# A residual stream kept token-major in a two-block model kernel: w_out and w_down with X stationary, sums of squares on ScalarE, transposes for the next X

## The chip, the cores and the metric

The kernel runs as one program on one core of one Trainium2 chip. The metric is the time of one execution on the device in microseconds (us); of several runs the median counts. Engines are named as in the profile: PE is TensorE (matmuls), PEld its weight load, DVE VectorE, ACT ScalarE, POOL GpSimd, SP SyncE, which here issues the DMAs. Matmul results land in PSUM, which has eight banks of 128 partitions x 512 fp32; everything else that is worked on lies in SBUF.

## The reference

Two blocks run one after the other on 256 tokens of width 1024, in fp32. The first has two layers; each adds a mixer and a gated feed-forward net to the residual stream `h`, behind an RMS norm each time:

```python
def rms_norm(x, g):
    y = x * rsqrt(mean(x * x, axis=-1) + EPS)
    return y * g

# first block, for layer in range(2):
xn   = rms_norm(h, attn_norm_g[layer])
proj = xn @ w_in[layer]                       # u, u_g, v_g, q, k, v
mixed = concat([s5_mixer(u), spatial_gating(u_g, v_g), diff_attention(q, k, v)])
h = h + mixed @ w_out[layer]                  # 1024 x 1024
xn = rms_norm(h, ffn_norm_g[layer])
a  = xn @ w_up[layer]                         # 1024 x 5632
a  = causal depthwise conv of width 3 (a) ; gate, val = split(a)
h  = h + (gelu(gate) * val) @ w_down[layer]   # 2816 x 1024

# second block:
hn = rms_norm_2(h, g_pre)
# three branches (dilated-window, grouped-query and memory attention), each with
# a silu gate and a product w_br, merged by sigmoid gates
merged = g0 * ya + g1 * yb + g2 * ym
x = h + rms_norm_2(merged @ w_out_2, g_post)
```

## The kernel before, in words

Each fp32 operand of a large product is split into a high part (rounded to the fp32r format) and a low part (the rest), and each product is three matmuls: high x high, high x low, low x high. Weights come as a stream in the fixed order of use (`Stream`): SP loads a piece of up to 128 x 2048 into a `wraw` buffer (3 of them), ACT copies its high part (`whi`, line 152), DVE subtracts for the low part (`wlo`, line 153); 5 buffers of each hold pieces of 128 x 1024. `st.take()` hands out the next piece and starts the split of later ones.

The input of a product is called X and is kept feature-major: tiles `xh` and `xl` of [128, 8, 256], that is 8 groups of 128 features on the partitions and the 256 tokens along the free axis. The residual stream `h` has the same layout. A product comes in two forms. With the weights stationary (`gemm_ws256`, and the loops of w_out and w_down) a 128 x 128 block of weights is loaded and the 256 tokens of X move through; the result is feature-major. With X stationary (`gemm_xs512`, and the final w_out_2) a 128 x 128 block of X is loaded and 512 columns of weights move through; the result is token-major, with 128 tokens on the partitions. X is not yet divided by the norm: the product's result is multiplied afterwards by the reciprocal root `rstd` of each token's mean square (`rb`, the same as a row broadcast over all partitions by two matmuls, for feature-major results).

w_out and w_down accumulate into four PSUM banks (`acc`), each with two groups of 128 features x 256 tokens; the loop runs over the pieces of weights and, inside, over banks, halves and the three products. In layer 0 the banks of w_out are first filled with x itself, by 16 products of x (`xraw`, token-major as it comes from memory) with the identity. Other products use two `ps` banks; one bank each, `pt` and `px`, takes transposes, sums and small things.

`residual` (line 1201) follows each of the four products w_out and w_down. It goes through the four banks: DVE adds the bank to `h` (line 1209), ACT makes the high part of the next X, scaled by the norm's gain (line 667), DVE the low part (line 668), ACT squares, DVE adds the two halves, and PE sums over the features by a product with a column of ones (`Stats.add`). `norm_from` turns the sums into `rstd` and `rb`.

The second block takes its tokens in a permuted order. The gated activations of layer 1's feed-forward net are written permuted (`up`, with `last`), so that w_down's result comes out permuted, and `residual` with `permute` copies `h` permuted. In the second block `x2_gen` transposes `h` back to token-major (16 transposes, four ACT copies) for the last addition, and the output rows are written through the view `(c b a) d -> a b c d`, which undoes the permutation.

Order: the code is written in the order of the computation, generators (`fill`, advanced by `step()`) put work of other parts between the pieces of a product, and the tile framework's scheduler orders each engine's instructions by the priority of the code's order, weight splits pushed back by `split_later`. Each engine then runs its own list strictly in order, and waits by semaphores for the others. The DMAs of weights and of the output are in SP's list.

## Time and profile before

| | |
|---|---|
| median of 3 runs | 1060.17 us (1058.84 to 1060.65) |
| the profiled execution | 1058.25 us, its span 1056.5 us |
| mean granted TensorE clock | 0.993 of full speed |
| PE busy | 1008.0 us, 95% of the span, 7943 matmuls |
| PEld busy | 934.4 us, 88% |
| DVE busy | 778.8 us, 74%, 1577 instructions |
| ACT busy | 624.6 us, 59%, 1206 instructions |
| memory traffic | 160.15 MB read, 1.05 MB written, 153 GB/s over the span |

All durations of single instructions come from the one profiled execution, which is 1.75 us longer than its span of work. Busy time of PE overlaps from one matmul to the next, since matmuls are pipelined, so the distance between starts (the pitch) tells what one costs. A window gives the busy time of each engine in a stretch; where PE's is as long as the window, PE never waits there. The chain of waits is followed back from the last instruction to what released each one.

### The profile page before, as it was taken

What the parts mean: (1) busy time and instruction counts of PE and PEld (TensorE: products, weight loads), DVE (VectorE), ACT (ScalarE), POOL (GpSimd) and SP (SyncE); (2) the same over time, 40 slices, a digit from 0 to 9 for tenths busy, and PEclk for the clock granted to TensorE, in tenths of its full rate; (3) what the DMA queues carried; (4) which work ended last, traced back from release to release, by engine and by line L of the source; (5) the groups of instructions that cost most, each with busy time, mean ns of one, the idle gap of its engine ahead of it and who ended that gap; (6) DMA issues with size and microseconds to landing.
All of it is one profiled execution on the core that took longest, in us unless ns stands there. A gap on an engine that the chain in (4) does not pass through costs nothing.

```text
span 1056.5 us, 20003 instructions
## 1 busy us (share of the span) xinstructions
PE 1008.0 (95%) x7943; PEld 934.4 (88%) x7943; DVE 778.8 (74%) x1577; ACT 624.6 (59%) x1206; POOL 14.3 (1%) x34
## 2 busy tenths in 40 slices
PE   6799899999999999998999999999999999999994
PEld 4678899999999988888999999998787899899993
DVE  6989869987888678768878778875565776456663
ACT  4886567656675577757555545646565545444450
POOL 2000000000000000000000000000000000000000
PEclk9999999999999999999999999999999999999997
DMA  6543253556555553253465656468323445325531
GB/s 191 194 160 132 71 187 107 176 191 220 182 186 171 182 169 122 80 193 127 161 202 172 206 172 203 138 196 282 108 98 110 148 144 188 117 90 194 174 126 40
DMA packets 130485, 166.68 MB, mean 158 GB/s; under 512 B 12034, under 2 KB 103256, under 8 KB 130392
## 3 DMA queue, kind: packets, MB, share of 16 engines
q1 hardware_dynamic: 130360, 165.40, 47.7%
q8 instruction: 62, 1.02, 0.4%
q14 instruction: 31, 0.25, 0.1%
q10 hardware_dynamic: 32, 0.01, 0.0%
HBM read 160.15 MB, written 1.05 MB: 153 GB/s over the span
## 4 chain that ended last, share of the span: by engine, by line
PE 79%; DVE 4%; ACT 3%; issue 1%; SPq 0%; DMA 0%; POOL 0%; ACTq 0%; POOLq 0%
PE acc L94 47%; PE ps L94 26%; DVE wlo L153 1%; PE pt L1509 1%; ACT whi L152 1%; PE px L94 1%; PE acc L1564 1%; PE acc L1655 1%; DVE sgen L409 1%; ACT sgen L600 1%; DVE gen L1334 0%; ACT gen L1008 0%; DVE gen L1336 0%; DVE gen L409 0%; PE acc L1566 0%
## 5 line engine op out<-in xcount | busy, mean ns | idle before, releaser
L152 ACT ACTIVATE whi<-wraw 128x1024 fp32r<-128x1024 f32 x294 | 307.9, 1061 | 231.5 <-PE acc L94 110.8
L153 DVE TENSOR_TENSOR wlo<-wraw,whi 128x1024 fp32r<-128x1024 f32 x294 | 356.6, 1223 | 102.1 <-ACT whi L152 99.4
L94 PE MATMUL ps<-xh,whi 128*128 128x256 f32 x736 | 208.7, 285 | 3.7 <-DVE gen L1345 3.4
L94 PE MATMUL ps<-xl,whi 128*128 128x256 f32 x736 | 208.2, 284 | 0.8 <-DVE xl L668 0.8
L94 PE MATMUL ps<-xh,wlo 128*128 128x256 f32 x736 | 207.9, 283 | 0.0
L94 PE MATMUL acc<-xh,wlo 128*128 128x256 f32 x672 | 193.6, 289 | 4.3 <-DVE wlo L153 4.3
L94 PE MATMUL acc<-xh,whi 128*128 128x256 f32 x672 | 194.4, 291 | 1.1 <-ACT vm L1198 0.7
L94 PE MATMUL acc<-xl,whi 128*128 128x256 f32 x672 | 193.4, 288 | 0.1
L94 PEld LDWEIGHTS ps<-xh,whi 128*128 128x128 f32 x736 | 140.5, 191 | 4.4 <-DVE gen L1345 1.9
L94 PEld LDWEIGHTS ps<-xl,whi 128*128 128x128 f32 x736 | 140.9, 192 | 1.1 <-DVE xl L668 1.0
L94 PEld LDWEIGHTS ps<-xh,wlo 128*128 128x128 f32 x736 | 140.9, 192 | 0.0
L94 PEld LDWEIGHTS acc<-xh,wlo 128*128 128x128 f32 x672 | 129.1, 192 | 6.5 <-DVE wlo L153 5.3
L94 PEld LDWEIGHTS acc<-xh,whi 128*128 128x128 f32 x672 | 129.0, 192 | 4.5 <-issue 1.3
L94 PEld LDWEIGHTS acc<-xl,whi 128*128 128x128 f32 x672 | 129.0, 192 | 2.4 <-issue 1.5
L94 PE MATMUL acc<-whi,xh 128*128 128x512 f32 (+1 forms) x352 | 125.1, 357 | 2.9 <-ACT xh L667 2.4
L94 PE MATMUL acc<-wlo,xh 128*128 128x512 f32 (+1 forms) x352 | 125.2, 356 | 1.7 <-DVE wlo L153 1.6
L94 PE MATMUL acc<-whi,xl 128*128 128x512 f32 (+1 forms) x352 | 124.2, 354 | 0.0
L94 PE MATMUL acc<-al,whi 128*128 128x256 f32 x352 | 99.0, 281 | 0.5 <-DVE al L672 0.5
L94 PE MATMUL acc<-ah,whi 128*128 128x256 f32 x352 | 99.1, 282 | 0.0
L94 PE MATMUL acc<-ah,wlo 128*128 128x256 f32 x352 | 98.6, 281 | 0.0
L94 PEld LDWEIGHTS acc<-whi,xh 128*128 128x128 f32 x352 | 67.1, 191 | 11.6 <-ACT xh L667 3.3
L94 PEld LDWEIGHTS acc<-wlo,xh 128*128 128x128 f32 x352 | 67.1, 191 | 10.4 <-DVE wlo L153 2.6
(348 smaller groups left out, 1517.2 us busy)
## 6 DMA issues: line engine op xcount, KB each, us to landing
wraw<-in_w_in_dram SPq DMA_DIRECT2D x58, 1024.0 KB
wraw<-in_w_up_dram SPq DMA_DIRECT2D x44, 1024.0 KB
wraw<-in_w_down_dram SPq DMA_DIRECT2D x22, 1024.0 KB
wraw<-in_w_out_dram SPq DMA_DIRECT2D x12, 1024.0 KB
wraw<-in_w_mem_kv_dram SPq DMA_DIRECT2D x4, 1024.0 KB
gen<-gen SPq DMA_DIRECT2D x48, 64.0 KB
wraw<-in_w_br_b_dram SPq DMA_DIRECT2D x2, 1024.0 KB
wraw<-in_w_br_m_dram SPq DMA_DIRECT2D x2, 1024.0 KB
```

What stands on the lines that cost most here:

```text
L94: self.nc.tensor.matmul(out, lhsT=lhsT, rhs=rhs, start=not self.open if start is None else start, stop=stop)
L152: self.nc.scalar.activation(hv, part, AF.Copy)
L153: self.nc.vector.tensor_tensor(lv, part, hv.bitcast(F32), op=OP.subtract)
L409: (eng or V).tensor_tensor(o, a, b_, op=op)
L600: A.copy(pd[ps, hf], bpow[ri][ps, a * 4 : a * 4 + 4])
L1509: T.transpose(bk.t[:, i * P : (i + 1) * P], p[:, i * P : (i + 1) * P], ident)
L1564: T.matmul(oc, lhsT=pt[:, kt * P : (kt + 1) * P], rhs=vs[0][:, kt, cols], start=kt == 0, stop=False)
L1655: T.matmul(oc, lhsT=pt[:, (i * 2 + kt) * P : (i * 2 + kt + 1) * P], rhs=vb[:, kt, kv * 64 : kv * 64 + 64], start=kt == 0, stop=kt == 1)
```

## The change

The residual stream stays token-major in `xraw`, where x is loaded, seen as `xrv`: 128 tokens on the partitions, two halves of tokens q, 1024 features. For this

- w_out and w_down are computed with X (the mixer's output, or the gated activations) stationary and 512 columns of weights moving (`mm_tok`); the four banks are two halves of tokens x two halves n of the features;
- `residual` adds each bank into `xrv` (DVE), squares with the row sum taken by the same ACT instruction, and makes the next feature-major X by 16 transposes on PE, from which ACT and DVE write the high and low parts, reading PSUM. The transposes go four at a time into the banks `pt` and `px` in turn;
- the products with ones, the products of x with the identity, and `x2_gen` are gone, and the last addition reads `xrv`;
- the permutation is made in the last residual, by transposes that write PSUM with a stride (`tokens`), with two more transposes for the norm; the gated activations are no longer permuted; the last merge adds with a permuted view, so that the product w_out_2 and the output are in the plain order, and each half of the output is one store of 128 rows in place of two of 64 rows in permuted order;
- `merged` moves from the pool of `h` to another, and the final store's view changes with it.

The core of the diff:

```diff
-    def norm_from(ss):
+    def tokens(ap, q, permute):
+        if not permute:
+            return ap[:, q * P : (q + 1) * P]
+        return flat_view(ap)[:, :, :, q * 8 : q * 8 + 8].rearrange("p a b c -> p c b a")
+
+    def norm_from(ss, permute=False):
...
-            T.matmul(bk.t[:, q * P : (q + 1) * P], lhsT=rstd[:, q : q + 1].to_broadcast([P, P]), rhs=ident,
+            T.matmul(tokens(bk.t[:, :S], q, permute), lhsT=rstd[:, q : q + 1].to_broadcast([P, P]), rhs=ident,
...
+        if permute:
+            bk = pst()
+            for q in range(2):
+                T.transpose(bk.t[:, q * P : (q + 1) * P], rb[:, q * P : (q + 1) * P], ident)
+            rstd = small.tile([P, 2], F32, name=nm("rstd"), tag="rstd", bufs=2)
+            A.copy(rstd, bk.t[:, :S].rearrange("p (q c) -> p q c", q=2)[:, :, 0])
...
-    def residual(banks, h, gcol, X, stats, permute=False, new=False):
-        for bi in range(4):
-            ks = slice(bi * 2, bi * 2 + 2)
-            hs = h[:, ks, :].rearrange("p k s -> p (k s)")
-            if new:
-                hv = banks[bi].t
-            else:
-                hv = gen() if permute else hs
-                V.tensor_tensor(hv, banks[bi].t, hs, op=OP.add)
-            for n in range(2):
-                k, x_ = bi * 2 + n, hv[:, n * S : (n + 1) * S]
-                split_scaled(X[0][:, k, :], X[1][:, k, :], x_, pcol(gcol + k))
-                if permute:
-                    A.copy(flat_view(h[:, k, :]), perm_view(x_))
-            sq = gen()
-            A.activation(sq, hv, AF.Square)
-            stats.add(sq)
-            if new:
-                A.copy(hs, hv)
+    def residual(banks, h, gcol, X, permute=False):
+        parts = sm(4)
+        for n in range(2):
+            for q in range(2):
+                hv = h[:, q, n * 512 : n * 512 + 512]
+                tt(hv, banks[q][n].t, hv, OP.add)
+                A.activation(gen(), hv, AF.Square, accum_out=parts[:, q * 2 + n : q * 2 + n + 1])
+            for kp in range(2):
+                bk = psx() if kp else pst()
+                for kk in range(2):
+                    k = n * 4 + kp * 2 + kk
+                    for q in range(2):
+                        T.transpose(tokens(bk.t[:, kk * S : (kk + 1) * S], q, permute), h[:, q, k * P : (k + 1) * P], ident)
+                for kk in range(2):
+                    k = n * 4 + kp * 2 + kk
+                    split_scaled(X[0][:, k, :], X[1][:, k, :], bk.t[:, kk * S : (kk + 1) * S], pcol(gcol + k))
...
+    def mm_tok(banks, rows, last):
+        for n in range(2):
+            cols = slice(n * 512, n * 512 + 512)
+            for i, (xh, xl, hi, lo) in enumerate(rows):
+                for q in range(2):
+                    tok = slice(q * P, (q + 1) * P)
+                    b = banks[q][n]
+                    b.mm(b.t, xh[:, tok], hi[:, cols])
+                    b.mm(b.t, xh[:, tok], lo[:, cols])
+                    b.mm(b.t, xl[:, tok], hi[:, cols], stop=last and i == 1)
...
-        banks = [acc() for _ in range(4)]
-        if l == 0:
-            for k in range(8):
-                for q in range(2):
-                    banks[k // 2].mm(banks[k // 2].t[:, (k % 2) * S + q * P : (k % 2) * S + (q + 1) * P],
-                                     xrv[:, q, k * P : (k + 1) * P], ident)
-            h = hpool.tile([P, 8, S], F32, name="h0", tag="h")
...
+        banks = [[acc(), acc()] for _ in range(2)]
+        for k in OUT_ORDER[l]:
+            rows = []
+            for kk in range(2):
+                hi, lo = st.take()
+                rows.append((mix[0][:, k + kk, :], mix[1][:, k + kk, :], hi[:, 0, :], lo[:, 0, :]))
+            mm_tok(banks, rows, k == OUT_ORDER[l][-1])
+            step(2)
...
-    fill.append(x2_gen())
...
-                    tt(mv, mv, y, OP.add)
+                    if bi_ == 2:
+                        mt = gen()
+                        for n in range(2):
+                            sl = slice(n * S, (n + 1) * S)
+                            tt(perm_view(mt[:, sl]), flat_view(mv[:, sl]), flat_view(y[:, sl]), OP.add)
+                        mv = mt
+                    else:
+                        tt(mv, mv, y, OP.add)
...
-    ov = out[0].rearrange("(c b a) d -> a b c d", b=4, a=4)
+    ov = out[0].rearrange("(q p) d -> q p d", p=P)
...
-        V.scalar_tensor_tensor(of, of, rs, x2[:, q], op0=OP.mult, op1=OP.add)
-        for al in range(2):
-            nc.sync.dma_start(ov[q * 2 + al], of[al * 64 : al * 64 + 64, :])
+        V.scalar_tensor_tensor(of, of, rs, xrv[:, q], op0=OP.mult, op1=OP.add)
+        nc.sync.dma_start(ov[q], of)
```

How the instructions stand on the engines is shown at two places. The first is the handover from w_out of layer 1 to the up-products that follow. Names: `acc` are the banks of w_out, `ps` those of the up-products, `xh` and `xl` the parts of X, `gen` scratch tiles, `ident` the identity. A row is line, operation, result and operands, shape, and how many in a row. On PE, before, from the last w_out matmul on:

```order
L94 MATMUL acc_5745<-xh_5441,wlo_5863 128x256
L94 MATMUL ps_6056<-xh_5978,whi_5892 128x256
L94 MATMUL ps_6124<-xh_5978,whi_5950 128x256
L94 MATMUL ps_6056<-xl_5979,whi_5892 128x256
...
L94 MATMUL ps_6124<-xh_5978,wlo_5951 128x256
L94 MATMUL px_5980<-ones,gen_5989 128x1 x2
L94 MATMUL ps_6056<-xh_5978,whi_5892 128x256
L94 MATMUL ps_6124<-xh_5978,whi_5950 128x256
```

On PE, after:

```order
L94 MATMUL acc_5386<-whi_5455,xl_5083 128x512
L1208 MATMUL pt_5532<-ident,xraw 128x128 x4
L1208 MATMUL px_5541<-ident,xraw 128x128 x4
L94 MATMUL ps_5599<-xh_5523,whi_5461 128x256
L94 MATMUL ps_5667<-xh_5523,whi_5495 128x256
L94 MATMUL ps_5599<-xl_5524,whi_5461 128x256
...
L94 MATMUL ps_5667<-xh_5523,whi_5495 128x256
L1208 MATMUL pt_5556<-ident,xraw 128x128 x4
L1208 MATMUL px_5565<-ident,xraw 128x128 x4
L94 MATMUL ps_5599<-xl_5524,whi_5461 128x256
```

The products with ones stood one pair at a time between the up-products; now two sets of eight transposes stand there, the second behind the eighth matmul of the up-products, into the same two banks as the first.

On DVE at the same place, before, from the first add of a w_out bank on:

```order
L1209 TENSOR_TENSOR gen_5981<-acc_5742,h_1637 128x512
L153 TENSOR_TENSOR wlo_6058<-wraw_5890,whi_6057 128x1024
L668 SCALAR_TENSOR_TENSOR xl_5979<-gen_5981,pvt,xh_5978 128x256 x2
L1209 TENSOR_TENSOR gen_5994<-acc_5743,h_1637 128x512
L409 TENSOR_TENSOR gen_5989<-gen_5989 128x256
L153 TENSOR_TENSOR wlo_6088<-wraw_5948,whi_6087 128x1024
L668 SCALAR_TENSOR_TENSOR xl_5979<-gen_5994,pvt,xh_5978 128x256 x2
L1209 TENSOR_TENSOR gen_6007<-acc_5744,h_1637 128x512
L409 TENSOR_TENSOR gen_6002<-gen_6002 128x256
L668 SCALAR_TENSOR_TENSOR xl_5979<-gen_6007,pvt,xh_5978 128x256 x2
```

And after, from the first add on (`xraw` is the stream):

```order
L407 TENSOR_TENSOR xraw<-acc_5383,xraw 128x512
L407 TENSOR_TENSOR xraw<-acc_5385,xraw 128x512
L407 TENSOR_TENSOR xraw<-acc_5384,xraw 128x512
L153 TENSOR_TENSOR wlo_5601<-wraw_5459,whi_5600 128x1024
L407 TENSOR_TENSOR xraw<-acc_5386,xraw 128x512
L666 SCALAR_TENSOR_TENSOR xl_5524<-pt_5532,pvt,xh_5523 128x256
L666 SCALAR_TENSOR_TENSOR xl_5524<-px_5541,pvt,xh_5523 128x256
L153 TENSOR_TENSOR wlo_5631<-wraw_5493,whi_5630 128x1024
L666 SCALAR_TENSOR_TENSOR xl_5524<-pt_5532,pvt,xh_5523 128x256
L666 SCALAR_TENSOR_TENSOR xl_5524<-px_5541,pvt,xh_5523 128x256
```

The four adds now come together, with one weight split among them, and the four low parts that are read from the first two transpose banks follow around a second weight split.

The second place is after w_down of layer 0, where the products of the memory keys (`ps` with `wlo`) stand between the residual and the first product of layer 1 (`acc` with `whi`). On PE, before, from the last product of the memory keys on:

```order
L94 MATMUL ps_4590<-xh_3486,wlo_4532 128x256
L94 MATMUL px_4652<-ones,gen_4658 128x1 x2
L94 MATMUL px_4652<-ones,gen_4668 128x1 x2
L94 MATMUL px_4652<-ones,gen_4678 128x1 x2
L94 MATMUL px_4652<-ones,gen_4688 128x1 x2
L94 MATMUL acc_4712<-whi_4561,xh_4650 128x512
L94 MATMUL acc_4712<-wlo_4562,xh_4650 128x512
```

On PE, after:

```order
L94 MATMUL ps_4221<-xh_3261,wlo_4163 128x256
L1208 MATMUL pt_4290<-ident,xraw 128x128 x4
L1208 MATMUL px_4299<-ident,xraw 128x128 x4
L94 MATMUL acc_4353<-whi_4192,xh_4281 128x512
L94 MATMUL acc_4353<-wlo_4193,xh_4281 128x512
...
L94 MATMUL acc_4354<-whi_4192,xh_4281 128x512
L1208 MATMUL pt_4314<-ident,xraw 128x128 x4
L1208 MATMUL px_4323<-ident,xraw 128x128 x4
L94 MATMUL acc_4353<-whi_4192,xl_4282 128x512
```

All products with ones stood ahead of the first wide matmul; now the first eight transposes do, and the second eight stand behind the ninth of the wide matmuls.

## Rows read from the trace of the kernel before

**Rows 1.** The page: busy time of PE; shares of the chain that ended last.
```profile
PE 1008.0 (95%) x7943; PEld 934.4 (88%) x7943; DVE 778.8 (74%) x1577; ACT 624.6 (59%) x1206; POOL 14.3 (1%) x34
...
PE 79%; DVE 4%; ACT 3%; issue 1%; SPq 0%; DMA 0%; POOL 0%; ACTq 0%; POOLq 0%
```

**Rows 2.** Windows: stretch, length, busy us (x instructions) per engine, clock, DMA share, GB/s.
```profile
472.00:490.00 18.00, 14.79 (x116) 13.85 (x114) 14.29 (x31) 13.75 (x23) 0.00 (x0) 1.00 0.42 142
490.00:656.50 166.50, 166.28 (x1393) 166.31 (x1394) 133.38 (x192) 93.59 (x121) 0.00 (x0) 1.00 0.54 181
669.00:708.00 39.00, 39.00 (x328) 38.59 (x326) 29.29 (x54) 20.23 (x29) 0.00 (x0) 1.00 0.58 174
```

**Rows 3.** Timeline of DVE and SP at the end; windows of the end and of x's load.
```profile
1043.94 1.28 DVE L1812 SCALAR_TENSOR_TENSOR o<-o,sm,x 128x1024 f32<-128x1024 f32 x1
1039.82 6.55 SPq L1814 DMA_DIRECT2D out_dram<-o  x4
...
1040.00:1041.00 1.00, 0.67 (x3) 0.20 (x2) 0.00 (x0) 0.30 (x1) 0.00 (x0) 1.00 0.00 0
1046.00:1055.00 9.00, 0.00 (x0) 0.00 (x0) 0.00 (x0) 0.00 (x0) 0.00 (x0) 0.50 0.24 86
1.70:6.50 4.80, 0.73 (x2) 0.36 (x2) 1.93 (x1) 0.77 (x1) 4.49 (x12) 1.00 0.79 299
```

**Rows 4.** Chain in order of time: start us, us, engine tile line xcount.
```profile
361.42 7.54 PE acc L94 x33
...
605.09 5.68 PE acc L94 x48
610.77 11.51 PE ps L94 x96
```

**Rows 5.** Timeline of PE, last 24 matmuls: first and last (start us, us, instruction).
```profile
1035.07 0.39 PE L94 MATMUL acc<-whi,xh 128*128 128x512 f32 x1
...
1040.28 0.39 PE L94 MATMUL acc<-whi,xl 128*128 128x512 f32 x1
```

**Rows 6.** Lines of PE: xcount | busy us, mean ns | idle before.
```profile
L94 PE MATMUL px<-ones,gen 128*128 128x1 f32 x64 | 8.1, 237 | 0.0
...
L94 PE MATMUL acc<-ident,xraw 128*128 128x128 f32 x32 | 4.6, 282 | 0.0
```

**Rows 7.** Timeline of PE, eight transposes of the x2 step and the next matmul.
```profile
680.85 1.09 PE L1443 MATMUL pt<-ident,h 128*128 128x128 f32 x8
681.70 0.36 PE L94 MATMUL acc<-xh,wlo 128*128 128x256 f32 x1
```

**Rows 8.** Lines of DVE and ACT that the handovers use.
```profile
L1209 DVE TENSOR_TENSOR h<-acc,h 128x512 f32<-128x512 f32 x8 | 5.3, 682 | 0.0
L668 DVE SCALAR_TENSOR_TENSOR xl<-ps,pvt,xh 128x256 fp32r<-128x256 f32 x8 | 3.6, 476 | 0.1
L153 DVE TENSOR_TENSOR wlo<-wraw,whi 128x1024 fp32r<-128x1024 f32 x294 | 356.6, 1223 | 102.1 <-ACT whi L152 99.4 <-PE pt L696 0.8
...
L667 ACT ACTIVATE xh<-ps,pvt 128x256 fp32r<-128x256 f32 x8 | 3.4, 469 | 1.0 <-PE ps L800 0.8 <-DVE xl L668 0.2
L1193 ACT COPY kmT<-ps 128x512 f32<-128x512 f32 x2 | 1.1, 567 | 0.0
```

**Rows 9.** Timeline of PE at two handovers; in brackets the wait and its releaser.
```profile
141.04 0.28 PE L94 MATMUL ps<-xh,whi 128*128 128x256 f32 x1
...
157.74 0.38 PE L94 MATMUL ps<-xh,whi 128*128 128x256 f32 x1 [1.68 <-DVE gen L1345]
...
471.75 0.40 PE L94 MATMUL ps<-xh,whi 128*128 128x256 f32 x2
...
490.22 0.35 PE L94 MATMUL ps<-xh,whi 128*128 128x256 f32 x1 [1.74 <-DVE gen L1345]
```

**Rows 10.** Windows: the one place inside the work where the clock fell.
```profile
41.00:45.00 4.00, 0.04 (x1) 0.00 (x0) 4.00 (x11) 3.83 (x10) 0.00 (x0) 0.95 0.08 22
45.00:48.00 3.00, 2.97 (x14) 2.97 (x15) 3.00 (x7) 2.96 (x16) 0.00 (x0) 0.50 0.01 3
```

More of the change, by code (lines that the diff above doesn't have):

```diff
@@ L1290, in layer @@
         low[0] = 0
[L1291 to L1310 removed]
+        banks = [[acc(), acc()] for _ in range(2)]
[6 more added lines that the diff above has]
+            step(2)
         last = l == LAYERS - 1
         X = new_x()
[L1313 to L1316 removed]
+        rstd, rb = residual(banks, h, FG + l * 8, X)
         rb2 = rb.unsqueeze(1).to_broadcast([P, 2, S])
         st.split_later = (SPLIT_F0, SPLIT_F1)[l]
[L1320 removed]
+        banks = [[acc(), acc()] for _ in range(2)]
         if not last:
@@ L1349, in up @@
             ac = gen()
-            if last:
-                for n in range(2):
-                    sl = slice(n * S, (n + 1) * S)
-                    tt(flat_view(ac[:, sl]), perm_view(g_[:, sl]), perm_view(v_[:, sl]), OP.mult)
-            else:
-                tt(ac, g_, v_, OP.mult)
+            tt(ac, g_, v_, OP.mult)
             ah = work.tile([P, 512], F32R, name=nm("ah"), tag="mid", bufs=5)
@@ L1363, in down @@
             subs = [st.take(), st.take()]
[L1364 to L1373 removed]
+            rows = []
+            for kk in range(2):
+                hi, lo = subs[kk]
+                sl = slice(kk * S, (kk + 1) * S)
+                rows.append((ah[:, sl], al[:, sl], hi[:, 0, :], lo[:, 0, :]))
+            mm_tok(banks, rows, j == 10)
             step()
@@ L1385, in layer @@
         Xo = new_x()
-        stats = Stats()
-        residual(banks, h, GP if last else AG + 8, Xo, stats)
-        return h, Xo, stats.finish()
+        return Xo, residual(banks, h, GP if last else AG + 8, Xo, last)
     def chain(*gs):
@@ L1396, in tile_model @@
     for l in range(LAYERS):
-        h, X, norm = layer(l, None if l == 0 else h, X, norm)
+        X, norm = layer(l, xrv, X, norm)
     b1.close()
@@ L1433, in tile_model @@
     V.tensor_scalar(rstdh, rstd, 0.5, None, op0=OP.mult)
-    x2 = const2.tile([P, 2, D], F32, name="x2")
-    def x2_gen():
-        for q in range(2):
-            for half in range(2):
-                bk = pst()
-                for k in range(4):
-                    T.transpose(bk.t[:, k * P : (k + 1) * P], h[:, half * 4 + k, q * P : (q + 1) * P], ident)
-                A.copy(x2[:, q, half * 512 : half * 512 + 512], bk.t)
-                yield
     def qt_tile():
```

47 lines of the change are left out of this document (5 added, 42 removed).

## The prediction

> **What bounds the kernel now.** I read the page's busy shares and the chain of waits first: TensorE (PE) is busy 95% of the span and holds 79% of the chain [rows 1]. The windows by stretch then say where it is not the limit. In the feed-forward stretch and at the start of the second block PE never waits, while VectorE (DVE) has a fifth of its time free [rows 2]. So a nanosecond taken from a matmul there shows in the time. PE loses time in three kinds of place. One is the mixers' own waits. The second is the handover from one product to the next: after w_out of layer 1, 18 us hold 14.79 us of PE work [rows 2]. The third is the end: the last DVE instruction is over at 1045.2 and the span ends at 1056.5, with PE idle [rows 3]. The sum below is made against the profiled execution, 1058.25 us; the median of the runs, 1060.17, lies 1.9 above it, and that is added at the end.
>
> **Width of the two products.** In w_out and w_down 256-column matmuls become half as many 512-column ones. The chain gives the pitch of the old form: 48 w_down matmuls in 5.68 us, 118.3 ns each; 96 of the same form in 11.51 us, 119.9 ns [rows 4]. The new form (X stationary, weights moving) exists already: the last 24 matmuls of the kernel start 23 pitches apart in 5.21 us, 226.5 ns, and a run of 33 amid busy DVE and ScalarE (ACT) took 7.54 us, 228.5 ns [rows 4, 5]. So a pair gives back 2 x 118.3 - 228.5 = 8 ns in w_down and 11 in w_out: the columns streamed stay the same, and only a fixed part of some 10 ns is paid once instead of twice. Pairs: w_down 2 layers x 11 x 24 = 528, w_out 2 x 96 = 192. 528 x 8.1 + 192 x 11.3 = 4.3 + 2.2 = 6.5 us, all on the path. Bounds: 0, if the wide form goes at 237 ns beside the splits; 8, at 226.5.
>
> **Removed from PE.** In layer 0 the 16 products with the identity that load x into the w_out banks (32 records, 4.6 us busy [rows 6], about 0.11 us apart) go. Most stood where PE waits for the attention chain anyway, so I count 2.0 us of 3.5 (bounds 1 and 3.5). The sums of squares by a ones column (64 records, 8.1 us busy [rows 6]) and the 16 transposes of the old x2 step go too; eight of these in a row took 0.85 us up to the next matmul, 0.106 us apiece [rows 7]. They are set against what the handovers gain.
>
> **Added, at the four handovers.** Each gets 16 transposes, 16 x 0.106 = 1.7 us, against 16 records of sums of squares, about the same; so the count is even and what matters is waiting. PE takes its instructions in the written order. The second eight transposes write into the same two PSUM banks as the first eight, so they wait until DVE has read four tiles out, and the rest of the next product is queued behind them, as is everything that reads it. After the last w_out matmul of layer 1 DVE still has one add (0.68), a weight split (1.22), two low parts (0.48 each), a weight split and two more low parts, as the order shows: 0.68 + 1.22 + 0.95 + 1.22 + 0.95 = 5.0 us [rows 8]. ACT's high parts (0.47 each [rows 8]) run beside. The second transposes then end near 5.5 us, and PE has done only 8 matmuls of the next product meanwhile. The other 88 take 10.5 us, the row sums' broadcast 0.2: 16.2 us until the third up-product can begin.
> - After w_out, layer 0: now 141.04 to 157.74, 16.7 us [rows 9]. Gain 0.5.
> - After w_out, layer 1: now 471.75 to 490.22, 18.5 us, the last 1.74 of it a wait for the norm's user on DVE, with the norm itself delayed by the ones products [rows 9]. The squares now come off ACT with their sum, eight copies of h are gone, and the norm is ready before the first bank is full. Gain 2.3.
> - After w_down, layer 0: the 96 matmuls of the memory keys stand ahead of all 16 transposes. An ACT copy of keys (0.57), a high and a low part [rows 8] stand before the first wide matmul may take its operands, some 1.4 us of which the first transposes cover 0.9. That costs 0.5; the next transposes find their banks read out, as four high parts and a low part end by 3.2 us. Loss 0.5.
> - After w_down, layer 1: PE does not wait today [rows 2]. 12 matmuls and 16 records, 3.2 us, become 5.5; two more transposes for the permuted norm 0.2; the old x2 transposes give back 1.7. Loss 0.8.
> Together a gain of 1.5. Bounds: a loss of 8 (2 us more at each place) to a gain of 7 (no waiting). The trace has no transpose that writes PSUM with a stride; the nearest row is the plain one, and I take 0.106; at four times that, the 18 strided ones would add 5.8.
>
> **A rule against the change.** The granted clock fell to 0.5, the 1.2 GHz level, in one place inside the work: PE was idle from 41 to 45, and from 45 to 48 it got through 14 matmuls where 25 would fit, a loss of about 1.3 us [rows 10]. In the gaps around 472 to 490 it stayed at 1.00 [rows 2]. The Trainium skill, "TensorE: Matmul & The Clock Gate", part 4 on transposes, says that transposes do not count as PE activity the way matmuls do; by it the handovers, now transposes and short waits, could drop the clock. The trace leaves this open, as no stretch of it holds mainly transposes; it is rival C.
>
> **Costed at nothing.** DVE's 16 adds replace 12 adds and 16 pair sums; ACT loses four copies of x2, eight permuted copies and four of h. DVE's free fifth in the feed-forward stretch covers the rest; uncovered, the four extra accumulator reads per handover would cost under 1 us each. Eight half-width permuted adds replace four full ones in the last merge, beside PE's gate products; uncovered, 4 x 0.7.
>
> **The end.** Now: the last scaling ends at 1045.2, SyncE (SP) issues the second pair of output DMAs, packets run through the whole of 1046 to 1055 at a DMA share of 0.24 and 86 GB/s, and the span ends at 1056.5: 11.3 us [rows 3]. A share of 0.24 is four of 16 engines. The order of the output rows is 4 x 4 x 16 there; after the change a store is 128 plain rows, as the loads of x are, and the stretch of those loads shows a share of 0.79 and 299 GB/s [rows 3]. So 512 KB take 1.75 us instead of the queue of 1 MB. From issue (1039.82) to the first packet pass 1.2 us (none before 1041) [rows 3], and 1.5 from the last packet to the end: 1.2 + 1.75 + 1.5 = 4.5. Gain 6.8. Bounds: 0, if a store to memory goes at 86 GB/s whatever its shape; 7, at four times 86.
> The Trainium skill, "DMA: Bandwidth & Descriptors", section on why a DMA increments its semaphore by 16, says that a transfer uses the largest number of engines up to 16 that divides the slowest dimension of both sides: 4 before, 16 after. The 0.24 agrees; the sum by this rule is the one I made from rows.
>
> **Sum.** 6.5 + 2.0 + 1.5 + 6.8 = 16.8. 1058.25 - 16.8 = 1041.4, and with the 1.9 of the runs 1043.4 us.
>
> **Rivals.** A: the store is limited by the memory and not by four engines; for it, all of the trace's wide transfers are loads. The gain falls to 10: 1050. B: the wide matmuls gain nothing, since the trace's chain of them is often interleaved and DVE writes weight parts at the same time; against it, the 33 at 228.5. 1050. C: the clock drops at each handover, 4 x 1.3: 1049. D, the slower side: in-order PE stands still behind the two transpose banks for the whole preparation of X. If none of it is hidden, a handover costs two adds 1.4, 16 transposes 1.7, eight high and low parts 7.6, two weight splits 2.4, 13.1 instead of 5.5, four times 7.6 more: 1074. It turns the sign from 4.7 us more per handover on. For it, these places hold little else for PE to do; against it, the first half's transposes and matmuls stand ahead, and the last matmuls of the first product (12 wide ones, 2.7 us) cover the first adds. E: neither the width nor the store does what it should and the handovers lose a few us: no change, 1058 to 1062.
>
> **Numbers.** Forecast 0.74 (its own range 1039 to 1048), A 0.08, B 0.06, C 0.05, D 0.04, E 0.03. The range to 1052 takes in A, B and C with the median's own spread of 1; below, no waiting at the handovers and 8 from the width give 1036 to 1037, and it begins at 1037. A measurement of this kernel tells about 0.2% from no change, 2 us. Faster 0.93, the same 0.03, slower 0.04.
>
> **What would show it.** The page: 720 fewer matmuls from the wide form, all w_down rows 128x512 at a pitch of 227 to 230. The windows: the wait for the norm in the up stretch of layer 1 gone, and a new one on PE ahead of the second transposes, released by DVE's low parts, of 1 to 3 us at each of three handovers. Granted clock 1.00 there. At the end, two stores, a DMA share far above 0.24, and 4 to 5 us from the last DVE instruction to the end of the span. Wrong it would be if the store still took 9 us, if the wide matmuls came at 236 ns, or if the waits ahead of the second transposes passed 5 us.

## The result

The changed kernel took 1048.46 us, the median of 4 runs (1047.36 to 1049.75), beside 1059.51 for the kernel before in the same comparison: 0.9896 of it, interval 0.9877 to 0.9915. Forecast were 1043.4 and a range of 1037 to 1052: 11.0 us faster instead of 16.8, two thirds of the forecast gain. The profiled execution took 1047.36, its span 1045.1, against 1058.25 and 1056.5 before.

PE's busy line and its share of the chain, which answer to [rows 1]:

```profile
PE 1001.7 (96%) x7177; PEld 893.2 (85%) x7177; DVE 772.0 (74%) x1561; ACT 618.0 (59%) x1207; POOL 14.5 (1%) x34
...
PE 82%; DVE 8%; ACT 6%; issue 2%; DMA 1%; SPq 0%; POOL 0%; ACTq 0%; DVEq 0%; POOLq 0%
```

766 matmul records fewer: 720 from the wide form, 64 sums of squares, 32 loads of x and 16 transposes of the x2 step gone, 66 transposes new. The columns streamed by the large products are the same in both traces, so each place of the work can be set against the same place in the other trace. The table gives when it is reached (us from the start of the span), what the stretch in front of it gained or lost, and the terms of the forecast that belong there (2.2 for w_out and 4.3 for w_down halved over the layers):

| up to | before | after | stretch | forecast |
|---|---|---|---|---|
| end of w_out, layer 0 | 141.04 | 139.77 | -1.3 | -3.1 |
| third up-product, layer 0 | 157.74 | 157.20 | +0.7 | -0.5 |
| end of w_down, layer 0 | 344.5 | 342.5 | -1.5 | -2.15 |
| layer 1's first products behind the residual | 369.0 | 367.8 | +0.8 | +0.5 |
| end of w_out, layer 1 | 471.75 | 470.30 | -0.2 | -1.1 |
| third up-product, layer 1 | 490.22 | 486.93 | -1.8 | -2.3 |
| end of w_down, layer 1 | 668.6 | 664.1 | -1.2 | -2.15 |
| last 24 matmuls | 1035.1 | 1031.1 | +0.5 | +0.8 |
| end of the span | 1056.5 | 1045.1 | -7.4 | -6.8 |

The end. The last scaling on DVE, the second store on SP, and the windows behind them; they answer to [rows 3]:

```profile
1039.94 1.29 DVE L1789 SCALAR_TENSOR_TENSOR o<-o,sm,xraw 128x1024 f32<-128x1024 f32 x1
1041.26 0.34 SPq L1790 DMA_DIRECT2D out_dram<-o  x1
```

```profile
1041.20:1042.00 0.80, 0.00 (x0) 0.00 (x0) 0.03 (x1) 0.00 (x0) 0.00 (x0) 0.50 0.00 0
1042.00:1044.10 2.10, 0.00 (x0) 0.00 (x0) 0.00 (x0) 0.00 (x0) 0.00 (x0) 0.50 0.64 254
```

From the end of DVE's instruction (1041.23) to the end of the span pass 3.9 us, not 11.3. No packet moves up to 1042; then the store is through within 2.1 us at a share of 0.64, before at 0.24. (Columns of windows as in [rows 2].)

The wide matmuls, which answer to [rows 4, 5]. Chain of waits (start, length, tile, count), one w_down step and the up-products before it; then PE's timeline, first and last of six matmuls of w_out in layer 1 and of twelve of w_down:

```profile
214.29 11.51 PE ps L94 x96
225.80 5.60 PE acc L94 x24
```

```profile
462.81 0.39 PE L94 MATMUL acc<-whi,xh 128*128 128x512 f32 x1
...
463.95 0.39 PE L94 MATMUL acc<-whi,xl 128*128 128x512 f32 x1
...
603.42 0.39 PE L94 MATMUL acc<-wlo,ah 128*128 128x512 f32 x1
...
605.99 0.40 PE L94 MATMUL acc<-whi,ah 128*128 128x512 f32 x1
```

w_out: (463.95 - 462.81) / 5 = 228 ns. w_down: (605.99 - 603.42) / 11 = 233.6, and 5.60 / 24 = 233.3. The same form through the same function comes 6 ns later in w_down. A pair there gives back 2 x 118.4 - 233.4 = 3.4 ns, not 8.1.

The handovers. PE at the one behind w_out of layer 0 and at the one of layer 1, from the first transposes to the third up-product (469.61 is the third last matmul of w_out); they answer to [rows 9]:

```profile
139.77 0.60 PE L1208 MATMUL pt<-ident,xraw 128*128 128x128 f32 x4
140.20 0.60 PE L1208 MATMUL px<-ident,xraw 128*128 128x128 f32 x4
142.11 0.50 PE L94 MATMUL ps<-xh,whi 128*128 128x256 f32 x2 [1.31 <-ACT xh L665]
...
144.06 0.50 PE L94 MATMUL ps<-xh,whi 128*128 128x256 f32 x2 [0.69 <-ACT xh L665]
144.67 0.63 PE L1208 MATMUL pt<-ident,xraw 128*128 128x128 f32 x4
...
157.20 0.36 PE L94 MATMUL ps<-xh,whi 128*128 128x256 f32 x1
...
469.61 0.39 PE L94 MATMUL acc<-whi,xh 128*128 128x512 f32 x1
...
470.30 0.60 PE L1208 MATMUL pt<-ident,xraw 128*128 128x128 f32 x4
...
472.02 0.50 PE L94 MATMUL ps<-xh,whi 128*128 128x256 f32 x2 [0.68 <-ACT xh L665]
472.74 0.38 PE L94 MATMUL ps<-xl,whi 128*128 128x256 f32 x1 [0.21 <-DVE xl L666]
...
473.97 0.50 PE L94 MATMUL ps<-xh,whi 128*128 128x256 f32 x2 [0.50 <-ACT xh L665]
474.74 0.63 PE L1208 MATMUL pt<-ident,xraw 128*128 128x128 f32 x4 [0.27 <-DVE xl L666]
475.21 0.60 PE L1208 MATMUL px<-ident,xraw 128*128 128x128 f32 x4
...
486.93 0.28 PE L94 MATMUL ps<-xh,whi 128*128 128x256 f32 x1
```

Two waits were in the forecast, the second transposes (DVE's low parts, 0.27 at 474.74) and what is queued behind them; they end at 145.6 and 475.6, 5.8 and 5.3 us after the first transposes began, forecast 5.5. But the wait of 1 to 3 us ahead of the second transposes, looked for at three handovers, is 0.27 at this one and nothing at the other three. A third wait was not in the forecast: PE has nothing between the first transposes and the first matmul that reads them, and waits 1.31 and 0.68 us for ACT's first high part, and again 0.69 and 0.50 for the second pair; at the handovers behind w_down it is 1.00 and 0.69. From the end of w_out to the third up-product it is 17.4 and 16.6 us; forecast were 16.2 for both.

The granted clock at the four handovers, and the window of layer 1 that stood in [rows 2]:

```profile
139.50:146.00 6.50, 4.37 (x30) 3.42 (x29) 6.09 (x14) 5.53 (x14) 0.00 (x0) 1.00 0.58 197
353.50:359.00 5.50, 4.50 (x30) 3.78 (x29) 2.89 (x6) 3.65 (x8) 0.00 (x0) 1.00 0.60 192
470.00:476.00 6.00, 4.34 (x30) 3.38 (x29) 5.80 (x14) 4.76 (x12) 0.00 (x0) 1.00 0.52 193
664.00:670.50 6.50, 5.37 (x39) 4.42 (x38) 6.30 (x15) 5.22 (x13) 0.00 (x0) 1.00 0.49 160
472.00:490.00 18.00, 16.93 (x134) 16.18 (x135) 13.93 (x31) 12.59 (x23) 0.00 (x0) 1.00 0.45 152
```

1.00 at each in this run. It was not so in every run. In three experiments below whose handovers hold the same instructions, the profiled run shows the clock at 0.50, the 1.2 GHz level, at one handover: in `pad_after` and `odd_x` behind w_out of layer 1 (473 to 476 and 475 to 478), in `ident_load` behind w_out of layer 0 (144 to 147). In `pad_before`, which is the kernel before with a pad, it fell at two, behind the second up-product of layer 0 and behind w_out of layer 1. `pad_after` ahead of the fall and in it, then the two falls of `pad_before`:

```profile
470.00:473.00 3.00, 1.67 (x8) 1.13 (x8) 3.00 (x6) 2.89 (x9) 0.00 (x0) 0.99 0.50 124
473.00:476.00 3.00, 2.64 (x13) 2.59 (x13) 1.98 (x9) 1.05 (x3) 0.00 (x0) 0.50 0.55 225
```

```profile
158.00:161.00 3.00, 3.00 (x16) 3.00 (x16) 3.00 (x8) 2.28 (x5) 0.00 (x0) 0.50 0.23 69
479.00:482.00 3.00, 3.00 (x17) 3.00 (x16) 1.88 (x4) 2.37 (x5) 0.00 (x0) 0.52 0.00 0
```

In `pad_after` the stretch from the first transposes to the third up-product took 17.8 us (468.91 to 486.69) where the changed kernel took 16.6: the fall cost about 1.1 us. The Trainium skill, "TensorE: Matmul & The Clock Gate", part 4 on transposes, says that a transpose does not count as PE activity the way a matmul does. No run here tells that apart from the waits that stand beside the transposes; the kernel before does not transpose the stream at its handovers, and in `pad_before` the clock fell there too. The window of 472 to 490 now holds 16.93 us of PE work in 18, before 14.79.

### The profile page after: what moved, and what is told of

Read it like the earlier page. It is cut to its first block, busy times and chain, and to the rows that moved or that the text cites. A ratio compares the mean times of both kernels' runs of the same rounds, so it can differ in the third digit from the quotient of the medians.

```text
span 1045.1 us, 18439 instructions
## 1 busy us (share of the span) xinstructions
PE 1001.7 (96%) x7177; PEld 893.2 (85%) x7177; DVE 772.0 (74%) x1561; ACT 618.0 (59%) x1207; POOL 14.5 (1%) x34
## 4 chain that ended last, share of the span: by engine, by line
PE 82%; DVE 8%; ACT 6%; issue 2%; DMA 1%; SPq 0%; POOL 0%; ACTq 0%; DVEq 0%; POOLq 0%
PE acc L94 48%; PE ps L94 26%; DVE sgen L407 2%; DVE wlo L153 2%; PE pt L1479 1%; ACT whi L152 1%; ACT sgen L598 1%; ACT gen L1002 1%; DMA wraw<-in_w_in_dram 1%; PE acc L1534 1%; PE acc L1625 1%; DMA wraw<-in_w_mem_kv_dram 1%; PE px L902 0%; DVE sgen L917 0%; PE acc L1536 0%
## 5 line engine op out<-in xcount | busy, mean ns | idle before, releaser
L94 PE MATMUL acc<-xh,wlo 128*128 128x256 f32 x544 | 158.1, 291 | 4.3 <-DVE wlo L153 4.3
L94 PE MATMUL acc<-xh,whi 128*128 128x256 f32 x544 | 158.5, 292 | 0.8 <-ACT xh L665 0.7
L94 PE MATMUL acc<-xl,whi 128*128 128x256 f32 x544 | 157.1, 289 | 0.1
L94 PE MATMUL acc<-whi,xh 128*128 128x512 f32 (+1 forms) x416 | 150.6, 365 | 4.7 <-ACT xh L665 3.4
L94 PE MATMUL acc<-wlo,xh 128*128 128x512 f32 (+1 forms) x416 | 151.2, 363 | 1.9 <-DVE wlo L153 1.8
L94 PE MATMUL acc<-whi,xl 128*128 128x512 f32 (+1 forms) x416 | 149.5, 362 | 0.0
L94 PEld LDWEIGHTS acc<-xh,whi 128*128 128x128 f32 x544 | 105.1, 194 | 3.2 <-issue 1.3
L94 PEld LDWEIGHTS acc<-whi,xl 128*128 128x128 f32 x416 | 79.0, 190 | 10.2 <-DVE xl L666 0.3
L94 PE MATMUL acc<-whi,ah 128*128 128x512 f32 x176 | 69.9, 397 | 0.3 <-ACT ah L669 0.3
L94 PE MATMUL acc<-wlo,ah 128*128 128x512 f32 x176 | 69.5, 395 | 0.0
```

The costliest lines, as they stand in the source:

```text
L94: self.nc.tensor.matmul(out, lhsT=lhsT, rhs=rhs, start=not self.open if start is None else start, stop=stop)
```

## The experiments

All ratios are against the kernel before of the same comparison, whose median lay between 1058.7 and 1060.1. Runs of one kernel spread over some 2 us, those of `tail_old` over 4.8; falls of the granted clock, at the handovers or at the place of the fourth group, are one cause of it.

**1. The store.** `tail_old` puts the old store back, `tail_four` cuts the new one into four.

```diff
# tail_old
-    ov = out[0].rearrange("(q p) d -> q p d", p=P)
+    ov = out[0].rearrange("(c b a) d -> a b c d", b=4, a=4)
-        nc.sync.dma_start(ov[q], of)
+        for al in range(2):
+            nc.sync.dma_start(ov[q * 2 + al], of[al * 64 : al * 64 + 64, :])
# tail_four: the same loop with ov[q][al * 64 : al * 64 + 64, :] of the new view
```

> The changed kernel with the old form of the output store alone put back: two stores of 64 rows per half, written through the 4 x 4 x 16 view. Its output rows land in the wrong (permuted) order; nothing else differs. Theory: the store's form set the end, so all that the end gained comes back: 10 to 11.5 us from the last DVE instruction to the end of the span, in place of 4.1 to 4.5, DMA share there 0.24; profiled time 1047.4 + 7 = 1054 to 1055. Rival (the end became shorter because the last stretch of DVE and SP was reordered, and the store goes at the memory's pace whatever its form): 1047 to 1048.5, the share far above 0.24.

> The changed kernel with each output store cut into two of 64 plain rows, so that there are four as before the change, but in plain order. Theory (the form of the destination, 4 x 4 x 16 rows, spread a store over four DMA engines): as the changed kernel, 4 to 5 us from the last DVE instruction to the end of the span, share well above 0.24; 1047 to 1050. Rival (the number of stores and their issue cost the time): 8 us or more there, 1051 or more.

`tail_old` took 1056.26 (0.9966, 0.9954 to 0.9978), 7.8 more than the changed kernel; `tail_four` 1048.41 in its one run. The window behind the last DVE instruction, of `tail_old` and then of `tail_four`:

```profile
1043.20:1051.80 8.60, 0.00 (x0) 0.00 (x0) 0.01 (x1) 0.00 (x0) 0.00 (x0) 0.50 0.24 94
```

```profile
1042.20:1045.20 3.00, 0.00 (x0) 0.00 (x0) 0.00 (x0) 0.00 (x0) 0.00 (x0) 0.50 0.71 178
```

Four stores in plain rows end 5.0 us after DVE (1041.20 to 1046.2), four in the old form 10.6 (1043.21 to 1053.8) at a share of 0.24. The form decides, not the count; four plain stores in place of two cost 1.1 us. Of the 7.8 us between the medians the end makes 6.7 (10.6 for 3.9); the profiled run of `tail_old` also came out of w_out of layer 0 2.4 us later, by a fall of the clock (fourth group). The Trainium skill, "DMA: Bandwidth & Descriptors", section on why a DMA increments its semaphore by 16, says that a transfer uses the largest number of engines up to 16 that divides the slowest dimension of both sides; for the old form that is four of 16, and the share of 0.24 agrees.

**2. Place in SBUF.** As the programs allocate them, X, weights and ah/al begin at 32, 32 and 0 bytes modulo 64 in the kernel before, and at 0, 0 and 32 in the changed one: a tile of 8 bytes (`ones`) ahead of them is gone, and all moved by 32 together. In both, X agrees with the weights and ah/al do not. `pad_after` and `pad_before` add 32 unused bytes ahead of the pool of ah and al, so that these agree too; `odd_x` makes the X of the up-products disagree.

```diff
# pad_after, pad_before
+    shift = const1.tile([P, 8], F32, name="shift")
+    V.memset(shift, 0.0)
     con = const1.tile([P, CX], F32, name="con")
# odd_x
-    def new_x():
-        xh = xpool.tile([P, 8, S], F32R, name=nm("xh"), tag="xh")
+    def new_x(odd=0):
+            x = xpool.tile([P, 8 * S + 16], F32R, name=nm(n), tag=n)
+            parts.append(x[:, odd : odd + 8 * S].rearrange("p (k s) -> p k s", k=8))
...
-        X = new_x()      # of the feed-forward net
+        X = new_x(8)
```

> The changed kernel with one unused tile of 32 bytes per partition ahead of the pool that holds the gated activations (ah, al), so that these stand 32 bytes further on; no instruction of the work differs (one small memset at the start). In the changed kernel the 512-column matmuls of w_down come every 233 ns, those of w_out and of the other products with X stationary every 227, beside the same busy engines. Theory (place in SBUF): ah and al begin at 32 modulo 64 bytes and the weights at 0, whereas xh, xl and the weights agree; with ah and al moved to 0 modulo 64 the pitch in w_down falls to 227 and 528 x 6 ns = 3.2 us go: 1044. Rival 1 (something that runs only in the feed-forward stretch, such as PSUM reads beside the matmuls): the pitch stays 233, the time 1047 to 1048. Rival 2 (another distance than modulo 64 decides): the pitch changes to something else, or not.

> The kernel before with the same unused tile of 32 bytes per partition ahead of the pool with ah and al; no instruction of the work differs. There ah and al, the moving operands of w_down, begin at 0 modulo 64 bytes and the weights at 32, and the 256-column matmuls of w_down come every 118.4 ns, those of the up-products, whose operands agree, every 119.9. Theory (place in SBUF): with ah and al moved to 32 the pitch of w_down becomes 119.9 as well, 1056 x 1.5 ns = 1.6 us more: 1059.9 in the profiled run. Rival (the order of operands or the stretch decides): 118.4 as before, 1058 to 1059.

> The changed kernel, with the X tiles 64 bytes longer, and with the X of the two up-products begun 32 bytes into its tile; all else begins where it did modulo 64 bytes. No instruction's order or count is changed on purpose. Moving ah and al by 32 bytes took the 512-column matmuls of w_down from 233 to 227 ns where they came to agree with the weights modulo 64, and the 256-column ones of the kernel before from 118 to 120. Theory (what counts is whether the stationary and the moving operand agree modulo 64 bytes: the narrow form is faster where they differ, the wide one where they agree): the 2112 narrow matmuls of the up-products go from 119.9 to 118.0 to 118.4 ns, 3.2 to 4 us less: 1044.5 to 1045.5. Rival (ah's and al's own places matter, by another bit of the address or by the pool they share): 119.9 as before, 1047 to 1049.

`pad_after`: 1045.17 (0.9867, 0.9853 to 0.9882), 3.3 less than the changed kernel. `pad_before`: 1062.52, one run. `odd_x`: 1043.58 (0.9851, 0.9838 to 0.9865), 4.9 less. The chain of waits of `pad_after`, of `pad_before` and of `odd_x`, one w_down step each, and for `odd_x` the up-products:

```profile
225.35 5.47 PE acc L94 x24
```

```profile
227.98 5.76 PE acc L94 x48
```

```profile
215.25 11.31 PE ps L94 x96
226.56 5.58 PE acc L94 x24
```

5.47 / 24 = 228 ns where it was 233; 5.76 / 48 = 120 where it was 118.4; 11.31 / 96 = 117.8 where it was 119.9. The step of w_down is 0.13 us shorter in `pad_after`, and 22 steps make 2.9 of its 3.3 us. But for one memset at the start of the padded kernels no instruction was added, taken or moved between engines, and the neighbours are as busy as before: where the operands lie in SBUF relative to each other moves the pitch of a matmul, by 2 ns for 256 columns and 6 for 512, and the other way round: the narrow form is the faster one where ah and al disagree with the weights, the wide one the slower. The rule that I had for it did not hold: in `odd_x` the wide matmuls with X (of w_in, w_out and the second block), whose X and weights still agree modulo 64, went from 227 to 232 ns (median of some 620), and the narrow ones of the second block, which I had not meant to touch, got faster too, by 1.8 ns (mean of some 1600). The longer X tiles also changed the distance in other bits; that this did it is not shown, and which bits count stays open. By these pitches the up-products make 2112 x 2.1 = 4.4 of the 4.9 us, an estimate, and the two side effects about cancel. Of the 4.2 us that `pad_before`'s run lies above the profiled run of before, the pitch explains 1.6. The two falls of the clock shown above account for the rest: from the third up-product of layer 0 to the fifth (157.58 to 176.45) it took 18.9 us where before took 17.5, and from w_out of layer 1 to the third up-product (473.46 to 493.37) 19.9 where before took 18.5.

**3. The handovers.** `early` puts the first transposes ahead of the last three wide matmuls of the product; `early_acc_pad` sends, besides, the second ones into accumulator banks.

```diff
# early, in mm_tok's last call
+            if n and res:
+                res.adds(0)
             for i, (xh, xl, hi, lo) in enumerate(rows):
                 for q in range(2):
+                    if n and res and (i, q) == (1, 1):
+                        res.turns(0)
# early_acc_pad, besides
-                bk = psx() if kp else pst()
+                bk = acc() if n else psx() if kp else pst()
```

> The changed kernel with the first eight transposes of each of the four residuals put ahead of the last three 512-column matmuls of the product instead of behind them; the adds and squares of that half are issued before the product's second half. Count and kind of instructions are the same. In the changed kernel PE waits at each handover for ACT's first high part behind the first transposes: 1.5, 1.2, 0.85 and 0.85 us. Theory (the chain transpose, high part, first matmul is exposed because nothing stands between): three wide matmuls, 0.7 us, now cover it, and DVE's reading out of the first two banks begins 0.7 us earlier, so the second transposes wait less too: 0.7 to 1.2 us per handover, 3 to 4.5 in all: 1043 to 1044.5. Rival (the handover is bound by DVE's chain of four adds, low parts and weight splits, which is as long as before): the wait only moves to the second transposes, gain under 1 us in all: 1046.5 to 1048.

> Both edits that gained, together: the first eight transposes of each residual ahead of the last three wide matmuls, and ah and al 32 bytes further on. Theory (they act in different places, the handovers and the w_down matmuls): the gains of 3.4 and 3.3 us against the changed kernel add up, 1041 to 1042.5. Rival (a shorter w_down takes its cover from DVE, and the handovers wait longer): under 5 us, 1043.5 or more.

> As the two edits together, and the second eight transposes of each residual go into two of the accumulator banks that the adds have just read out, in place of the two banks of the first eight. Theory (the second transposes wait for DVE to read the first four tiles out): they can follow the adds at once, the waits of 0.3 to 0.9 us ahead of them at each handover go, 1 to 3 us in all: 1039 to 1041. Rival (by then PE waits for DVE's adds and ACT's high parts, not for the banks; and w_down's accumulators, which follow in the same rotation, come later): no change, 1041 to 1043.

`early`: 1045.02 (0.9864, 0.9849 to 0.9878), 3.4 less than the changed kernel and 0.5 above its theory's range. `early_pad` (with the 32 bytes): 1042.07 (0.9839, 0.9824 to 0.9853), the two gains added up. `early_acc_pad`: 1039.66 (0.9816, 0.9802 to 0.9829), another 2.4. PE of `early` behind w_out of layer 1:

```profile
470.37 0.60 PE L1215 MATMUL pt<-ident,xraw 128*128 128x128 f32 x4
...
471.70 0.39 PE L94 MATMUL acc<-whi,xl 128*128 128x512 f32 x1
471.93 0.40 PE L94 MATMUL ps<-xh,whi 128*128 128x256 f32 x2
472.84 0.39 PE L94 MATMUL ps<-xl,whi 128*128 128x256 f32 x1 [0.51 <-DVE xl L666]
...
473.81 0.50 PE L94 MATMUL ps<-xh,whi 128*128 128x256 f32 x2 [0.24 <-ACT xh L665]
...
486.67 0.28 PE L94 MATMUL ps<-xh,whi 128*128 128x256 f32 x1
```

The first up matmul follows the last wide one without a wait. In its place stand 0.51 us for DVE's low part at 472.84: DVE, not ACT, is late next. With the second transposes in banks of their own, the same handover in `early_acc_pad`, from the first transposes to the third up-product:

```profile
466.54 0.60 PE L1217 MATMUL pt<-ident,xraw 128*128 128x128 f32 x4
...
482.19 0.28 PE L94 MATMUL ps<-xh,whi 128*128 128x256 f32 x1
```

That is 15.7 us; in `early` it is 16.3 (470.37 to 486.67). Both hold the last three wide matmuls behind the first transposes; the changed kernel, counted from where these three begin (469.61 to 486.93), takes 17.3 for the same work.

**4. What stood ahead of w_out in layer 0.** `ident_load` puts the products of x with the identity back; `early_single_pad` goes through w_out's pieces one at a time.

```diff
# ident_load
+        if l == 0:
+            for n in range(2):
+                for q in range(2):
+                    for k in range(4):
+                        c = n * 512 + k * P
+                        banks[q][n].mm(banks[q][n].t[:, k * P : (k + 1) * P], ident, xrv[:, q, c : c + P])
# early_single_pad, in the loop over kk
+                if k != OUT_ORDER[l][-1]:
+                    mm_tok(banks, rows, False)
+                    rows = []
+                    step()
```

> The changed kernel with the load of x into the w_out banks of layer 0 put back, as 16 products with the identity of 128 columns each (and a copy out in place of DVE's add). Everything else as changed. Forecast counted 2.0 us for their removal. Theory 1 (they cost what they take on PE where nothing covers them): 1 to 2 us more, 1049 to 1050.5. Theory 2 (they stand in the waits of the attention chain ahead of w_out, where the changed kernel has PE busy 1.17 of 3 us, and in some executions the granted clock falls to 0.50 just behind, at 117 to 124 us; with them the stretch holds more PE work): the chain takes the same time, the executions with the fall become rarer, and the median falls to about the 1047.4 of the runs without it, or below 1048.

> As the two edits together, and in w_out the pieces of weights are gone through one at a time (but for the last pair), not two at a time with the halves of the columns outside. Count of matmuls the same. Theory (the pair makes the first piece's second half wait for the second piece, so that PE has less to do in the waits of the attention chain of layer 0, 105 to 120 us, where the changed kernel loses 1 to 2 us more than the kernel before): 0.5 to 2 us less than both edits together, PE busier than 1.17 of 3 us at 114 to 117. Rival (the chain of attention sets the time there whatever PE has to do): the same within 0.5 us.

`ident_load`: 1047.0 (1045.5 to 1047.9; 0.9882, 0.9868 to 0.9896), not slower than the changed kernel but 1.5 us faster, its interval overlapping. The 2.0 us forecast for taking the load out were not there: in the profiled runs w_out of layer 0 ends at 139.75 with the load and at 139.77 without, both with the clock at 1.00 ahead of it. The number that its second theory gave was met, but not shown is the reason, that falls of the clock become rarer. `early_single_pad`: 1042.51 (0.9844), the same as `early_pad`: the rival held. PE and the clock at 114 to 117, of the changed kernel, of `ident_load`, and at the same place a little later in the profiled run of `early`:

```profile
114.00:117.00 3.00, 1.17 (x69) 0.99 (x72) 2.99 (x20) 0.53 (x3) 0.00 (x0) 1.00 0.00 0
```

```profile
114.00:117.00 3.00, 1.88 (x120) 1.72 (x120) 2.88 (x18) 0.16 (x2) 0.00 (x0) 1.00 0.02 5
```

```profile
117.00:120.00 3.00, 2.35 (x55) 1.81 (x44) 1.58 (x4) 0.69 (x1) 0.00 (x0) 0.50 0.02 5
120.00:123.00 3.00, 3.00 (x19) 2.35 (x12) 0.62 (x1) 1.88 (x2) 0.00 (x0) 0.50 0.00 0
123.00:126.00 3.00, 3.00 (x13) 2.54 (x13) 0.75 (x1) 0.71 (x2) 0.00 (x0) 0.87 0.00 0
```

In the changed kernel PE has 1.17 us of work in these 3, with the load back 1.88. And here the clock can fall: in the profiled run of `early` it stood at 0.50 from 117 to past 123, and that run came out of this stretch 2.1 us later than the changed kernel's, whose profiled run kept 1.00. The trace of `tail_old` shows the same fall, 2.4 us late; those of `odd_x` and `early_acc_pad` a shorter one (0.53 and 0.51 in 117 to 120, 1.00 behind it), and `early_acc_pad` came out only 0.2 us late. How much work PE has at 114 to 117 does not tell the runs with a fall from those without: `early` had 1.50 us and fell, `early_acc_pad` 1.80 and fell, the changed kernel 1.17 and kept 1.00.

Of the changed kernel's four runs two had a mean clock of 0.994 and took 1047.4 and 1047.5, and two 0.991 and took 1049.4 and 1049.8. So its median of 1048.46 probably holds a part of such falls, which its profiled run does not. Only the mean clock is known of the runs without a trace; whether they fell here or at a handover is not shown. Of `ident_load`'s four, one had 0.992 and three 0.994 or 0.995; its profiled run kept 1.00 here and fell at a handover. Four runs are too few to say that the load prevents a fall.

**5. All together.** `best` is `early_acc_pad` with the X of the up-products moved and the load of x put back.

> All edits that gained, together: first transposes ahead of the last three wide matmuls, second transposes into accumulator banks, ah and al 32 bytes further on, the X of the up-products 32 bytes into its tile, and the load of x by products with the identity put back in layer 0. Theory (all act in different places): 1039.7 less 3.2 to 4 for the up-products, less 0 to 1.4 for the identity products: 1034.5 to 1036.5. Rival (DVE, with less time per up-product, becomes late for the weights' low parts): 1037 or more.

1033.54 (1033.46 to 1034.25; 0.9759, 0.9746 to 0.9772): 14.9 us below the changed kernel and 25 below the one before, 1.0 us better than its expectation, a rest that no run takes apart. Its trace has no fall of the clock from 51 us to the end of the matmuls, and its five runs have mean clocks of 0.994 to 0.997, so a part of the 14.9 may be falls in the changed kernel's median. One w_down step and the up-products behind it, chain of waits:

```profile
207.75 5.47 PE acc L94 x24
213.21 11.31 PE ps L94 x96
```

## Why the prediction was right, and where it was off

The time lies in the range that takes in the rivals, but 0.5 us above the forecast's own 1039 to 1048, close to the times given to rivals A to C (1049 to 1050). Which terms held is read from the traces, not from that number.

- **The end: right.** Forecast 6.8, measured 7.4; 6.7 when undone, by the traces. Rival A is out.
- **Width: right in w_out, under half in w_down.** The pitch of 228.5 was read off a product whose X lies otherwise to the weights than w_down's ah and al do; w_down came at 233. 528 pairs at 3.4 ns make 1.8 us instead of 4.3 (its stretches gained 2.7 in all; the other 0.9 is not taken apart). The same places had made the narrow form cheap before, 118.4 against 119.9: the old form was read where it is at its best, the new one then ran where it is at its worst. With 32 bytes put in, the forecast pitch appeared, worth 2.9 us, and the median fell by 3.3. Rival B (nothing gained, for DVE's writing) is out: 228 beside the same writing.
- **The load of x: wrong.** The step "most stood where PE waits for the attention chain anyway, so I count 2.0 us of 3.5" took a share where there was none. All of it stood there: put back, it moved the end of w_out by nothing (139.75 and 139.77). With it gone PE is emptier where the clock can fall, but that this makes it fall is not shown.
- **The handovers: right in kind, too good in size.** The second transposes ended when forecast, to 0.3 us. What failed is "PE has done only 8 matmuls of the next product meanwhile. The other 88 take 10.5 us": the eight themselves waited, for ACT's high part behind the first transposes. Forecast a gain of 1.5 over the four, measured a loss of 0.2: +0.7 for -0.5, +0.8 for +0.5, -1.8 for -2.3, +0.5 for +0.8 in the table. `early` shows that the wait for the high part was real and could be covered: 3.4 us.
- **Rival C** did not happen as placed, at each handover: the changed kernel's profiled run has 1.00 at all four. But it was no idle rival. In the profiled runs of `pad_after`, `odd_x` and `ident_load` the clock fell at one handover, at about 1.1 us for the forecast 1.3, and in some runs at a fifth place, ahead of w_out in layer 0, at 0.2 to 2.4 us. The falls at the handovers are not new: `pad_before` has two. The 1.9 us by which the median of before lay above its profiled run fit them (a mean clock of 0.990 or 0.991 in most of its runs, 0.993 in the profiled one), but those runs have no trace. **Rival D** did not happen. Nor did transposes with a stride cost more; the first eight of the last residual, from PE's timeline:

```profile
664.14 0.60 PE L1208 MATMUL pt<-ident,xraw 128*128 128x128 f32 x4
664.58 0.60 PE L1208 MATMUL px<-ident,xraw 128*128 128x128 f32 x4
```

  Four in 0.44 us, 0.11 apiece, as the plain ones at 139.77.
- **Sum.** By the table the spans differ by 11.4 for a forecast of 16.8. Short by 1.8 up to the end of w_out in layer 0, 1.6 in w_down, 1.7 at the handovers and 0.9 in layer 1's mixer; 0.6 more than forecast at the end. The mixer's 0.9 stands where ACT waits for a weight piece, in the changed kernel's profiled run and then in that of `ident_load`, which did not lose the time:

```profile
412.86 1.06 ACT L152 ACTIVATE whi<-wraw 128x1024 fp32r<-128x1024 f32 x1 [1.24 <-DMA wraw<-in_w_mem_kv_dram]
```

```profile
412.13 1.06 ACT L152 ACTIVATE whi<-wraw 128x1024 fp32r<-128x1024 f32 x1 [0.18 <-DMA wraw<-in_w_mem_kv_dram]
```

  From SP's issue of that load (406.64 and 406.97) it is 6.2 and 5.2 us; in the kernel before ACT does not wait there. The attention that ACT does next came later by it, and w_out with it. Why the load took longer stays open.

## What to carry to other kernels

A pitch read off one product holds for another only where the operands lie alike in SBUF: look at their places before carrying it over, and try a pad of 32 bytes. When work is taken out of a stretch in which an engine waits, count nothing for it until the chain that it waits for gets shorter. When a step makes an operand by way of a second engine (transpose, split, multiply), ask what the first engine does between the first transpose and its first reader, and put the last matmuls of the old product there.

## What the runs showed of the hardware

The pitch of a matmul depends on where its operands begin in SBUF: 256 columns at 117.8 or 119.9 ns, 512 at 227 to 228 or 232 to 233, with the same code beside the same neighbours; 32 bytes of padding were worth 2.9 us here by the pitch, 3.3 between the medians, and moving the X of the up-products 4.9 with its side effects. One and the same move can help one form and hurt another: it sped the wide w_down up and slowed the narrow one of the kernel before from 118.4 to 120.

The granted clock can fall to 0.50 behind a stretch in which PE waits, and the same instructions can pass there at 1.00 in another run: at a handover the fall cost 1.1 to 1.4 us (`pad_after`, `pad_before`), with transposes in the stretch or without. One profiled run does not show whether the next run has such a fall; look at the mean clock of every run before explaining a difference of 1 or 2 us.
